# A two-layer mixer and expert trunk on one core: elementwise work goes from POOL to VectorE and ScalarE, the second layer's router sums move among the first layer's experts, and the first gather is split between the first expert products

## The chip, the cores and the metric

The kernel runs on one core of one Trainium2 chip. The core's engines work in parallel and each takes its own instructions in order: TensorE (PE; its weight loads are listed apart as PEld), VectorE (DVE), ScalarE (ACT), GpSimd (POOL) and SyncE (SP), which here issues the large transfers to 16 DMA engines. An instruction waits on semaphores for what it needs, and everything queued behind it on its engine waits too. The metric is device time in microseconds (us), the median of three runs: 862.81 us (861.21 to 863.67). A difference of 0.3% is about what a measurement of this kernel can tell.

## What is computed

Two layers over 256 tokens of 1024 channels, all in float32. A layer projects its input, runs four token mixers, gates and merges them, normalises, and then sends each token to two of 32 experts. Cut to what matters here:

```python
for l in range(DEPTH):                                   # 2 layers
    z = h @ w_in[l]                                      # 1024 -> 2560 + 4 * 1024 gate logits
    branches = (short_conv(sc_b, sc_c, sc_x, ...),       # gated convolution
                rg_lru(lru_x, ...),                      # recurrence over the tokens
                spatial_gating(sg_u, sg_v, ...),         # standardised in groups of 64, then a causal product
                retention(r_q, r_k, r_v, r_g, ...))      # rotated q and k, standardised output, silu gate
    merged = sum(sigmoid(gate_logits[b]) * (branches[b] @ branch_proj[l, b]) for b in range(4))
    mix = merged @ w_out[l]
    h = layer_norm(ALPHA * h + mix, ln_mix_g[l], ln_mix_b[l])
    ffn = hier_moe(h, ...)    # router: group by softmax, top 2 of its 8 experts; expert: silu(h wg) * (h wu) wd
    h = layer_norm(ALPHA * h + ffn, ln_ffn_g[l], ln_ffn_b[l])
```

## The kernel before

Weights come in chunks of 1 MB, 34 for a layer's mixers and 96 for its experts (8 groups of 4 experts, 12 chunks each: 8 for gate and up, 4 for down). A ring of 22 slots of 1 MB holds the chunks in flight and a few larger buffers. `Ring.pump` issues the next load from SyncE whenever a slot has been given back; the loads go out in the fixed order of the list, with a few others hung before certain chunks (`before`): the mixers' parameters `par` and the router's `rp` come before chunk 4 of layer 2.

**Mixers.** The products must be exact to float32, so each operand is split into a high half (ScalarE's cast, L256) and the rest (VectorE's subtraction, L257), and three products take the place of one (L328 to L330). A quarter of a chunk, 128x512, is a *piece*. A layer's mixers have 136, numbered from 0: ten chunks of input projections (q, k, lx, v, g, sv, su, c, x, b), then gates, branch projections (`proj`) and output projections in turn. A piece is 12 products (6 in the output projections). Splits run four pieces ahead (LOOK): the split for piece u + 4 is issued after the products of piece u, into the slot of the low halves (`wlo`) that piece u has just left. So VectorE can't run further ahead than that.

The mixers themselves are generators: after each piece, `advance` takes every one of them a step further, to its next `yield`. What a generator issues in a step stands in the engines' queues right behind that piece. A `yield` more or less thus moves all of its later work by one piece of 12 products. `g_ret` (retention), `g_lru` (recurrence) and `g_sgu` (spatial gating) use `std64`, which standardises over groups of 64 columns; its inverse root is found by `rsqrt`, 12 small steps on POOL (L315 to L318) on eight columns. The larger elementwise operations that don't read PSUM stand on POOL: the rotation's sum (L573), the retention output's two products (L620, L621) ahead of its transposes (L628), the recurrence's (L663, L673), the spatial gating's subtraction (L537) and products (L697, L714) around its products `sv` (L705).

**Residual and router sums.** After the first gate `residual` scales h by ALPHA on POOL; in layer 2 it first loads the norm's gain and bias (`gb`), scales them, and multiplies and adds them to h: five operations of 1024 or 2048 columns on POOL. `g_router` then puts the norm's gain into the router's weights `wr` and sums them with TensorE (L286, L296).

**Norm and routing.** `norm_mix` adds the residual, transposes the sums, and finds the router's logits from the sums themselves; mean and deviation are put in afterwards (L835, L838). Both token halves' logits share one PSUM bank; VectorE copies one half (L824), ScalarE the other (L825). `route` picks groups and experts, and makes one-hot matrices.

**Experts.** For a group, `gather` makes the tokens' columns (`xg`, L1151) by products with the one-hot matrices, a half of the channels (4 blocks) a call and 2 blocks a step. The first group's gather stands ahead of the first expert product (L1052): three of its four steps, and the fourth behind the weight k = 3. Each `gu` product of a chunk gives its slot back to the ring.

## Time and profile before

| | |
|---|---|
| median of 3 runs | 862.81 us |
| span of the profiled execution, first to last instruction | 860.7 us |
| mean granted TensorE clock | 0.970 of full speed |
| busy: TensorE, its weight loads, VectorE, ScalarE, POOL | 92%, 70%, 45%, 37%, 14% |
| layer 1: mixers to about 225 us, experts to about 425 us | |
| layer 2: mixers to about 652 us, experts to about 850 us | |
| read from HBM | 278.85 MB, 325 GB/s over the span |

The profile is of one execution, whose own time besides the span isn't listed; the span is 2.1 us under the median. A busy share of 92% on TensorE doesn't say that TensorE is the bound throughout: records of waiting products overlap, and in the experts its weights arrive one at a time. A granted clock of 1.00 is 2.4 GHz, 0.50 is 1.2 GHz; values between are means over a window. A row's bracket says how long the engine sat idle ahead of it and what ended that.

### The profile page before, as it was taken

Reading aid. Unit: us, or ns where it says so; the run is one execution under the profiler, and the core shown is the slowest. Engines: PE = TensorE matmul, PEld = TensorE weight load, DVE = VectorE, ACT = ScalarE, POOL = GpSimd, SP = SyncE. Lnnn points to the kernel's source line nnn. Section 1 sums busy time; section 2 is a strip of 40 time slices with the busy share of each in tenths; the row PEclk is TensorE's granted clock in tenths of the full one; section 3 lists DMA queues with packets and bytes.
Section 4 is the critical chain, followed back from the end, with each engine's and each line's share of the span. In section 5 each row is a group of like instructions: output and inputs, shape, how many; then the busy total and the mean of one; then the engine's idle time right before and its main releaser. Section 6 shows DMA issues by size and latency. Waiting matters only on the chain.

```text
span 860.7 us, 15923 instructions
## 1 busy us (share of the span) xinstructions
PE 791.3 (92%) x6438; PEld 604.1 (70%) x6438; DVE 386.0 (45%) x732; ACT 317.3 (37%) x636; POOL 124.8 (14%) x153
## 2 busy tenths in 40 slices
PE   8999999999999999867889998999999999979794
PEld 7998999999656555422389988999995565544342
DVE  5778677466621111110386779665674211111004
ACT  6564444444523211110356633544444131112012
POOL 4526211011000000000131437110010000000001
PEclk9999999999999999988999999999999999997898
DMA  9986735557799999999997474555587999999994
GB/s 346 425 354 264 253 122 179 191 196 280 323 424 426 426 426 425 425 421 425 424 425 303 158 281 164 183 196 191 175 334 320 426 426 426 425 426 427 423 425 175
DMA packets 40823, 281.07 MB, mean 327 GB/s; under 512 B 4588, under 2 KB 4588, under 8 KB 7456
## 3 DMA queue, kind: packets, MB, share of 16 engines
q1 hardware_dynamic: 40320, 279.20, 80.9%
q8 instruction: 54, 0.88, 0.4%
q10 hardware_dynamic: 288, 0.52, 0.2%
q0 software_dynamic: 128, 0.19, 0.1%
q14 instruction: 33, 0.27, 0.1%
HBM read 278.85 MB, written 1.05 MB: 325 GB/s over the span
## 4 chain that ended last, share of the span: by engine, by line
PE 58%; DMA 27%; DVE 7%; ACT 2%; POOL 1%; issue 1%; SPq 0%; DVEq 0%; ACTq 0%; POOLq 0%
DMA w<-in_exps_dram 25%; PE z L328 9%; PE z L330 9%; PE z L329 9%; PE gu L1052 6%; PE xg L1151 3%; PE y L1102 3%; PE acc L1089 3%; DVE wlo L257 2%; PE pj L330 2%; PE pj L328 2%; PE pj L329 2%; PE acc L328 2%; PE acc L329 2%; PE acc L330 2%; DMA par<-in_par_dram 2%
## 5 line engine op out<-in xcount | busy, mean ns | idle before, releaser
L257 DVE TENSOR_TENSOR wlo<-w,whi 128x512 fp32r<-128x512 f32 x269 | 215.7, 825 | 115.7 <-ACT whi L256 71.6
L330 PE MATMUL z<-hThi,wlo 128*128 128x256 f32 x672 | 192.2, 286 | 3.2 <-DVE wlo L257 3.0
L328 PE MATMUL z<-hThi,whi 128*128 128x256 f32 x672 | 192.5, 286 | 0.4 <-ACT whi L256 0.4
L329 PE MATMUL z<-hTlo,whi 128*128 128x256 f32 x672 | 191.3, 285 | 0.0
L256 ACT CAST whi<-w 128x512 fp32r<-128x512 f32 x272 | 151.4, 618 | 13.4 <-PE z L329 6.7
L1052 PE MATMUL gu<-w,xg 128*32 128x512 f32 x1024 | 128.0, 635 | 22.2 <-PEq L1175 13.0
L330 PEld LDWEIGHTS z<-hThi,wlo 128*128 128x128 f32 x672 | 130.1, 194 | 4.9 <-DVE wlo L257 4.9
L328 PEld LDWEIGHTS z<-hThi,whi 128*128 128x128 f32 x672 | 130.3, 194 | 1.2 <-ACT whi L256 0.7
L329 PEld LDWEIGHTS z<-hTlo,whi 128*128 128x128 f32 x672 | 130.2, 194 | 0.2
L1052 PEld LDWEIGHTS gu<-w,xg 128*32 128x32 f32 x1024 | 30.4, 114 | 98.2 <-issue 65.3
L1157 ACT ACTIVATE xg<-xg,cst 128x128 f32<-128x128 f32 x64 | 25.8, 454 | 167.2 <-PE xg L1151 163.9
L1159 DVE TENSOR_SCALAR xg<-xg,cst 128x128 f32<-128x128 f32 x64 | 23.3, 405 | 129.7 <-PE xg L1151 129.7
L1102 PE MATMUL y<-w,hidT 128*32 128x256 f32 x1024 | 65.4, 383 | 12.8 <-ACT hidT L1082 10.8
L1151 PEld LDWEIGHTS xg<-oh,h 128*128 128x128 f32 x512 | 59.6, 191 | 24.4 <-issue 22.7
L1089 PE MATMUL acc<-y,ct 128*128 128x256 f32 x256 | 68.1, 398 | 1.0 <-ACT y L1106 1.0
L1151 PE MATMUL xg<-oh,h 128*128 128x128 f32 x512 | 65.4, 281 | 0.0
L1089 PEld LDWEIGHTS acc<-y,ct 128*128 128x128 f32 x256 | 44.7, 189 | 25.0 <-issue 11.9
L1102 PEld LDWEIGHTS y<-w,hidT 128*32 128x32 f32 x1024 | 28.9, 109 | 41.1 <-ACT hidT L1082 14.6
L488 POOL TENSOR_TENSOR late<-late 128x512 f32<-128x512 f32 x16 | 25.9, 1616 | 203.9 <-DVE late L483 184.7
L1128 DVE TENSOR_TENSOR ow<-oh,wt 128x256 f32<-128x256 f32 x16 | 6.8, 424 | 106.9 <-PE y L1102 78.8
L1106 ACT COPY y<-y 128x256 f32<-128x256 f32 x64 | 23.8, 373 | 78.6 <-PE y L1102 78.6
L401 ACT ACTIVATE late<-z 128x512 f32<-128x512 f32 x32 | 19.1, 597 | 90.6 <-PE z L330 90.6
(257 smaller groups left out, 1044.4 us busy)
## 6 DMA issues: line engine op xcount, KB each, us to landing
w<-in_exps_dram SPq DMA_DIRECT2D x190, 1024.0 KB, 19.5
w<-in_mixw_dram SPq DMA_DIRECT2D x66, 1024.0 KB, 8.0
w<-in_mixw_dram SPq DMA_DIRECT2D x8, 256.0 KB, 6.2
par<-in_par_dram SPq DMA_DIRECT2D x2, 1024.0 KB, 15.9
w<-in_exps_dram SPq DMA_DIRECT2D x4, 512.0 KB, 17.7
xT<-in_xT_dram SPq DMA_DIRECT2D x4, 256.0 KB, 5.4
h<-in_xtok_dram SPq DMA_DIRECT2D x1, 1024.0 KB, 18.2
gb<-in_fgb_dram SPq DMA_DIRECT2D x1, 1024.0 KB, 5.8
```

The costliest lines, as they stand in the source:

```text
L256: self.nc.scalar.copy(hi, src)
L257: (eng or self.nc.vector).tensor_sub(lo, src, hi.bitcast(F32))
L328: nc.tensor.matmul(out, ah, bh, start=first and i == 0, stop=False, skip_group_check=True)
L329: nc.tensor.matmul(out, ah, bl, start=False, stop=False, skip_group_check=True)
L330: nc.tensor.matmul(out, al, bh, start=False, stop=stop_last and i == n - 1, skip_group_check=True)
L488: nc.gpsimd.tensor_add(a, a, pr)
L1052: nc.tensor.matmul(bank[32 * c:32 * c + 32], xg[g][k // 4][:, k % 4, 32 * c:32 * c + 32], w[:, c], start=k == 0, stop=k == 7, skip_group_c ...
L1089: nc.tensor.matmul(self.W[t][half][:, c0:c0 + 256], ct[:, t * P:t * P + P], y, start=g == 0 and c0 == 0, stop=g == 7, skip_group_check=True)
L1102: nc.tensor.matmul(bank[32 * c:32 * c + 32], hidT[:, f * P + 32 * c:f * P + 32 * c + 32], w[:, f, c], start=f == 0, stop=f == 1, skip_grou ...
L1106: nc.scalar.copy(ys[q], bank)
L1151: nc.tensor.matmul(bank[:, i * P:i * P + P], self.h[:, t, k * P:k * P + P], oh[:, t].rearrange("p e s -> p (e s)"), start=t == 0, stop=t == 1)
L1157: nc.scalar.activation(x[:, 2 * j + i], bank[:, i * P:i * P + P], AF.Identity, bias=b, scale=g)
```

## The change

- *POOL's large operations in the mixers* go to VectorE: L537, L573, L620 and L621 (in the other order), L663, L673, L697, L714. With them some `yield`s go: the retention transposes stand two pieces earlier, and so do the `sv` products.
- *The residual* becomes a generator, `g_residual`. Layer 1: four scalings of 512 columns on ScalarE, one a piece. Layer 2: the load at the same place, 14 pieces later four scalings of `gb` on ScalarE, then eight operations of 512 columns on VectorE, one every two pieces; the slot of `gb` is given back at its end.
- *Layer 2's router sums* run after group 6 of layer 1's experts, in PSUM banks of another kind. Their parameters `rp` are loaded ahead of chunk 56 of layer 1's experts, no more among layer 2's mixer chunks.
- *Routing*: the two halves' logits get a bank each, ScalarE copies both; mean and deviation are put together (`lm`) ahead of the logits, one step instead of two behind them; the value `nm` is made on POOL.
- *First gather*: two steps ahead of the first expert product, one each behind the weights k = 0 and k = 1.

The change also drops comments. The core of it:

```diff
+            before[(l - 1) * NCH + NMIX + 56] = [(self.router_params, l)]
...
                         if (j, bp) == (0, 0):
-                            self.residual(l)
-                            self.gens.append(self.g_router(l))
-                        if (j, bp) == (4, 0) and l:
-                            ring.give()
+                            self.mgens.append(self.g_residual(l))
+                            if l == 0:
+                                self.gens.append(self.g_router(l))
...
-        (nc.gpsimd if d is src else nc.vector).tensor_tensor(v3(d), v3(src), s[:, :, None].to_broadcast([P, 8, 64]),
-                                                             op=OP.subtract)
-        yield
-        if d is src:
-            yield
+        nc.vector.tensor_tensor(v3(d), v3(src), s[:, :, None].to_broadcast([P, 8, 64]), op=OP.subtract)
+        yield
...
-            nc.gpsimd.tensor_add(A, A, B)
+            nc.vector.tensor_add(A, A, B)
...
-        yield
-        nc.gpsimd.tensor_tensor(v3(d), v3(d), rs[:, :, None].to_broadcast([P, 8, 64]), op=OP.mult)
-        nc.gpsimd.tensor_mul(d, d, sl)
-        for _ in range(4):
+        nc.vector.tensor_mul(d, d, sl)
+        yield
+        nc.vector.tensor_tensor(v3(d), v3(d), rs[:, :, None].to_broadcast([P, 8, 64]), op=OP.mult)
+        for _ in range(2):
             yield
...
-        nc.gpsimd.tensor_mul(i, i, xc)
+        nc.vector.tensor_mul(i, i, xc)
...
-        nc.gpsimd.tensor_mul(r, r, i)
-        yield
+        nc.vector.tensor_mul(r, r, i)
...
-        nc.gpsimd.tensor_tensor(v3(vg), v3(vg), rs[:, :, None].to_broadcast([P, 8, 64]), op=OP.mult)
-        for _ in range(3):
+        nc.vector.tensor_tensor(v3(vg), v3(vg), rs[:, :, None].to_broadcast([P, 8, 64]), op=OP.mult)
+        for _ in range(2):
             yield
...
-        nc.gpsimd.tensor_mul(o, o, ug)
-        yield
+        nc.vector.tensor_mul(o, o, ug)
...
-        rb = self.bank("B", "rt")
+        rbt = [self.bank("W", "rt")[:, :P] for _ in range(2)]
...
-        self.stats_end(0)
+        self.recip(0)
         self.stats_var(1)
-        self.stats_end(1)
-        lt = self.tt("lt", [P, T])
-        nc.vector.tensor_copy(lt[:, :P], rb[:, :P])
-        nc.scalar.copy(lt[:, P:], rb[:, P:256])
+        lt = [self.tt("lt", [P, P]) for _ in range(2)]
+        for t in range(2):
+            nc.scalar.copy(lt[t], rbt[t])
...
         for t in range(2):
-            nc.vector.scalar_tensor_tensor(lm[:, t], self.rbs[:, 0], self.mv[:, t, 0:1], raw[:, t],
+            nc.vector.tensor_scalar(lm[:, t], self.rbs[:, 0], self.mv[:, t, 0:1], None, op0=OP.mult)
+        self.recip(1)
+        for t in range(2):
+            nc.vector.scalar_tensor_tensor(lm[:, t], lm[:, t], self.rs[:, t:t + 1], self.rbs[:, 1],
                                            op0=OP.mult, op1=OP.add)
-        for t in range(2):
-            nc.vector.scalar_tensor_tensor(lg[:, t], lm[:, t], self.rs[:, t:t + 1], self.rbs[:, 1],
+            nc.gpsimd.tensor_scalar(self.nm[:, t:t + 1], self.mv[:, t, 0:1], -1.0, None, op0=OP.mult)
+            nc.gpsimd.tensor_mul(self.nm[:, t:t + 1], self.nm[:, t:t + 1], self.rs[:, t:t + 1])
+        for t in range(2):
+            nc.vector.scalar_tensor_tensor(lg[:, t], raw[:, t], self.rs[:, t:t + 1], lm[:, t],
                                            op0=OP.mult, op1=OP.add)
...
+    def g_residual(self, l):
...
         if l == 0:
-            nc.gpsimd.tensor_scalar(self.h, self.h, ALPHA, None, op0=OP.mult)
+            for i in range(4):
+                yield
+                nc.scalar.mul(rows[:, 512 * i:512 * i + 512], rows[:, 512 * i:512 * i + 512], ALPHA)
             return
...
-        nc.gpsimd.tensor_scalar(gb, gb, ALPHA, None, op0=OP.mult)
-        for t in range(2):
-            nc.gpsimd.tensor_mul(self.h[:, t], self.h[:, t], gb[:, :1024])
-            nc.gpsimd.tensor_add(self.h[:, t], self.h[:, t], gb[:, 1024:])
+        for _ in range(14):
+            yield
+        for i in range(4):
+            nc.scalar.mul(gb[:, 512 * i:512 * i + 512], gb[:, 512 * i:512 * i + 512], ALPHA)
+            yield
+        for i in range(4):
+            c = slice(512 * (i % 2), 512 * (i % 2) + 512)
+            x = rows[:, 512 * i:512 * i + 512]
+            nc.vector.tensor_mul(x, x, gb[:, c])
+            yield
+            yield
+            nc.vector.tensor_add(x, x, gb[:, 1024 + c.start:1024 + c.stop])
+            yield
+            yield
+        self.ring.give()
...
-        next(first[1])
...
-                if (g, k) == (0, 3):
+                if g == 0 and k < 2:
                     next(first[1], None)
...
+            if g == 6 and l + 1 < L:
+                for _ in self.g_router(l + 1, "B"):
+                    pass
```

Where the changed file's line numbers differ, its rows below carry its own. VectorE in layer 1's mixers, from the variance of the spatial gating (`sbs`) to the transposed retention rows: before, five splits in a row and then the short convolution.

```order
L545 TENSOR_REDUCE sbs<-sgu 128x8
L546 TENSOR_SCALAR sbs<-sbs 128x8
L311 TENSOR_SCALAR ris<-sbs 128x8
L312 TENSOR_SCALAR rys<-ris 128x8
L257 TENSOR_TENSOR wlo<-w,whi 128x512 x5
L727 TENSOR_TENSOR sc<-z,sc 128x512
```

In the changed kernel, the same place on VectorE:

```order
L546 TENSOR_REDUCE sbs<-sgu 128x8
L547 TENSOR_SCALAR sbs<-sbs 128x8
L316 TENSOR_SCALAR ris<-sbs 128x8
L317 TENSOR_SCALAR rys<-ris 128x8
L258 TENSOR_TENSOR wlo<-w,whi 128x512 x2
L620 TENSOR_TENSOR ret_238<-ret_238 128x512
L258 TENSOR_TENSOR wlo<-w,whi 128x512
L622 TENSOR_TENSOR ret_238<-ret_238,ryr 128x512
L258 TENSOR_TENSOR wlo<-w,whi 128x512 x2
L697 TENSOR_TENSOR sgu<-sgu,rys 128x512
```

Three products that POOL had stand between the splits now; two of them read POOL's inverse roots (ryr, rys). The same engine a little earlier, from the retention's standardisation (`sar`) on; before:

```order
L537 TENSOR_TENSOR ret_238<-ro,sar 128x512
L672 SCALAR_TENSOR_TENSOR lru<-lru 128x512
L257 TENSOR_TENSOR wlo<-w,whi 128x512 x2
L545 TENSOR_REDUCE sbr<-ret_238 128x8
L546 TENSOR_SCALAR sbr<-sbr 128x8
```

In the changed kernel:

```order
L541 TENSOR_TENSOR ret_238<-ro,sar 128x512
L673 SCALAR_TENSOR_TENSOR lru<-lru 128x512
L674 TENSOR_TENSOR lru<-lru 128x512
L258 TENSOR_TENSOR wlo<-w,whi 128x512
L677 SCALAR_TENSOR_TENSOR lru<-lru 128x256 x2
L258 TENSOR_TENSOR wlo<-w,whi 128x512
L546 TENSOR_REDUCE sbr<-ret_238 128x8
```

The recurrence's product (L674) and its scans (L677) have moved ahead of the variance `sbr`. TensorE at the start of layer 1's experts, gather (`xg`) and the first products (`gu`); before:

```order
L1151 MATMUL xg<-oh,h 128x128 x12
L1052 MATMUL gu<-w,xg 32x512 x16
L1151 MATMUL xg<-oh,h 128x128 x4
L1052 MATMUL gu<-w,xg 32x512 x8
L1151 MATMUL xg<-oh,h 128x128 x8
```

In the changed kernel:

```order
L1173 MATMUL xg<-oh,h 128x128 x8
L1071 MATMUL gu<-w,xg 32x512 x4
L1173 MATMUL xg<-oh,h 128x128 x4
L1071 MATMUL gu<-w,xg 32x512 x4
L1173 MATMUL xg<-oh,h 128x128 x4
L1071 MATMUL gu<-w,xg 32x512 x16
```

The first expert product stands behind 8 gather products instead of 12 (each is two records in the trace, 16 instead of 24).

## Rows read from the trace of the kernel before

**Rows 1.** The page, part 2: GB/s in 40 equal slices of the span.

```profile
GB/s 346 425 354 264 253 122 179 191 196 280 323 424 426 426 426 425 425 421 425 424 425 303 158 281 164 183 196 191 175 334 320 426 426 426 425 426 427 423 425 175
```

**Rows 2.** The chain of waits, 330 to 440 us: start, us, what.

```profile
336.28 19.53 DMA w<-in_exps_dram
...
439.19 0.12 PE z L328
```

**Rows 3.** Windows of 1 us: PE, PEld, DVE, ACT, POOL busy, clock, DMA share, GB/s.

```profile
234.00:235.00 1.00, 1.00 (x14) 0.27 (x10) 0.09 (x1) 0.97 (x3) 0.00 (x0) 1.00 0.00 0
235.00:236.00 1.00, 1.00 (x16) 0.38 (x12) 0.00 (x0) 1.00 (x1) 0.00 (x0) 1.00 0.83 123
```

**Rows 4.** Timeline of TensorE and SyncE, start of layer 1's experts: start, us, what.

```profile
230.40 2.92 PE L1151 MATMUL xg<-oh,h 128*128 128x128 f32 x24
233.25 3.21 PE L1052 MATMUL gu<-w,xg 128*32 128x512 f32 x28
...
234.38 5.84 SPq L116 DMA_DIRECT2D w<-in_exps_dram  x6
```

**Rows 5.** Timeline of TensorE's weight loads in the mixers.

```profile
64.17 0.19 PEld L330 LDWEIGHTS z<-hThi,wlo 128*128 128x128 f32 x1 [0.44 <-DVE wlo L257]
...
73.78 0.42 PEld L628 LDWEIGHTS rtp<-cst,ret 128*128 128x128 f32 x4 [2.31 <-POOL ret L621]
...
89.15 0.19 PEld L330 LDWEIGHTS z<-hThi,wlo 128*128 128x128 f32 x1 [0.65 <-DVE wlo L257]
...
529.48 0.19 PEld L330 LDWEIGHTS z<-hThi,wlo 128*128 128x128 f32 x1 [1.30 <-DVE wlo L257]
```

**Rows 6.** Windows of 2 and of 10 us in the mixers, columns as above.

```profile
76.00:78.00 2.00, 2.00 (x11) 2.00 (x11) 1.34 (x2) 0.00 (x0) 1.23 (x2) 0.50 0.00 0
...
150.00:160.00 10.00, 10.00 (x85) 10.00 (x85) 4.14 (x7) 3.97 (x9) 0.00 (x0) 1.00 0.61 210
...
520.00:530.00 10.00, 8.77 (x71) 8.37 (x70) 9.88 (x7) 4.48 (x9) 9.76 (x5) 1.00 0.34 120
```

**Rows 7.** Timeline of VectorE, then POOL, in layer 1's mixers.

```profile
56.44 2.47 DVE L257 TENSOR_TENSOR wlo<-w,whi 128x512 fp32r<-128x512 f32 x2
...
63.42 2.14 DVE L257 TENSOR_TENSOR wlo<-w,whi 128x512 fp32r<-128x512 f32 x2
66.22 0.69 DVE L257 TENSOR_TENSOR wlo<-w,whi 128x512 fp32r<-128x512 f32 x1 [0.66 <-ACT whi L256]
...
68.05 3.10 DVE L257 TENSOR_TENSOR wlo<-w,whi 128x512 fp32r<-128x512 f32 x5
...
60.21 0.51 POOL L315 TENSOR_TENSOR rzr<-ryr 128x8 f32<-128x8 f32 x1 [1.84 <-DVE ryr L312]
60.79 0.50 POOL L316 TENSOR_TENSOR rzr<-rzr,sbr 128x8 f32<-128x8 f32 x1
...
75.41 0.20 POOL L316 TENSOR_TENSOR rzs<-rzs,sbs 128x8 f32<-128x8 f32 x1
...
84.54 5.75 POOL L922 TENSOR_SCALAR h<-h 128x2048 f32<-128x2048 f32 x1
```

**Rows 8.** The chain of waits in layer 2's mixers: the router sums.

```profile
511.40 1.02 PE rb L286 x16
516.92 0.56 PE rb L296 x4
```

**Rows 9.** A weight load in group 7; then the DMA issues, KB and us to landing.

```profile
397.75 0.16 PEld L1052 LDWEIGHTS gu<-w,xg 128*32 128x32 f32 x8 [1.70 <-DMA w<-in_exps_dram]
...
rp<-in_rp_dram SPq DMA_DIRECT2D x1, 384.5 KB, 15.7
```

**Rows 10.** Timeline of ScalarE and VectorE at layer 1's routing.

```profile
225.55 0.27 ACT L825 COPY lt<-rt 128x128 f32<-128x128 f32 x1 [0.68 <-DVE lt L824]
...
226.32 0.42 DVE L835 SCALAR_TENSOR_TENSOR lm<-rbs,mv,lg 128x40 f32<-128x40 f32 x2 [0.86 <-PE lg L828]
...
227.00 0.28 DVE L940 MAX8 top<-lg 128x8 f32<-128x8 f32 x2
```

More of the change, by code (lines that the diff above doesn't have):

```diff
@@ L257, in hilo, with router_params @@
         (eng or self.nc.vector).tensor_sub(lo, src, hi.bitcast(F32))
+    def router_params(self, l):
+        rp = self.lp.tile([P, 769], F32, name="rp")
+        self.nc.sync.dma_start(rp, self.a["rp"][l])
+        self.bsb = rp[:, :256].rearrange("p (c t) -> p c t", c=2)
+        self.wr = rp[:, 256:768].rearrange("p (k e) -> p k e", k=8)
+        self.rb = rp[:, 768:]
     def params(self, l):
-        nc, a, lp = self.nc, self.a, self.lp
+        nc, a = self.nc, self.a
         par = self.ring.take("par")
@@ L268, in params @@
         nc.sync.dma_start(par, a["par"][l])
-        rp = lp.tile([P, 769], F32, name="rp")
-        nc.sync.dma_start(rp, a["rp"][l])
-        self.bsb = rp[:, :256].rearrange("p (c t) -> p c t", c=2)
-        self.wr = rp[:, 256:768].rearrange("p (k e) -> p k e", k=8)
-        self.rb = rp[:, 768:]
+        if l == 0:
+            self.router_params(l)
     def done_with_params(self):
@@ L278, in done_with_params, with g_router @@
             self.ring.give()
-    def g_router(self, l):
+    def g_router(self, l, tag="W"):
         nc = self.nc
         gb = self.col(l, "mg", 0, 16).rearrange("p (i k) -> p i k", i=2)
-        bank = self.bank("W", "rb")
+        bank = self.bank(tag, "rb")
         for k in range(8):
@@ L293, in g_router @@
         yield
-        bank = self.bank("W", "rb")
+        bank = self.bank(tag, "rb")
         for i in range(2):
@@ L403, in mixer @@
                         if (j, bp) == (0, 0):
-                            self.residual(l)
-                            self.gens.append(self.g_router(l))
-                        if (j, bp) == (4, 0) and l:
-                            ring.give()
+                            self.mgens.append(self.g_residual(l))
+                            if l == 0:
+                                self.gens.append(self.g_router(l))
                         if (j, bp) == (7, 1):
@@ L764, in stats_var, with recip @@
         nc.scalar.activation(self.sd[:, t:t + 1], self.mv[:, t, 1:2], AF.Sqrt, bias=self.eps)
+    def recip(self, t):
+        self.nc.vector.reciprocal(self.rs[:, t:t + 1], self.sd[:, t:t + 1])
     def stats_end(self, t):
         nc = self.nc
-        nc.vector.reciprocal(self.rs[:, t:t + 1], self.sd[:, t:t + 1])
+        self.recip(t)
         nc.vector.scalar_tensor_tensor(self.nm[:, t:t + 1], self.mv[:, t, 0:1], -1.0, self.rs[:, t:t + 1],
@@ L797, in logits @@
                 o = i % 2 * 64
-                nc.tensor.matmul(rb[o:o + 64, t * P:t * P + P], self.wr[:, 4 * q + i], xT[t, q][:, i],
-                                 start=t + q == 0 and i < 2, stop=q == 1 and i > 1, skip_group_check=True)
+                nc.tensor.matmul(rbt[t][o:o + 64, :], self.wr[:, 4 * q + i], xT[t, q][:, i],
+                                 start=q == 0 and i < 2, stop=q == 1 and i > 1, skip_group_check=True)
         for t in range(2):
@@ L819, in norm_mix @@
         self.stats_add(1, 1, part(1, 1))
-        self.stats_end(0)
+        self.recip(0)
         self.stats_var(1)
-        self.stats_end(1)
-        lt = self.tt("lt", [P, T])
-        nc.vector.tensor_copy(lt[:, :P], rb[:, :P])
-        nc.scalar.copy(lt[:, P:], rb[:, P:256])
+        lt = [self.tt("lt", [P, P]) for _ in range(2)]
+        for t in range(2):
+            nc.scalar.copy(lt[t], rbt[t])
         raw = self.bank("W", "lg")[:, :80].rearrange("p (t e) -> p t e", t=2)
         for t in range(2):
-            nc.tensor.matmul(raw[:, t], lt[:, t * P:t * P + P], self.cst[:, C_SEL:C_SEL + 40], start=True, stop=True)
+            nc.tensor.matmul(raw[:, t], lt[t], self.cst[:, C_SEL:C_SEL + 40], start=True, stop=True)
         yield
@@ L915, in norm_ffn @@
             self.do_split(u)
-    def residual(self, l):
+    def g_residual(self, l):
         nc = self.nc
         self.needs[self.layer] -= 1
+        rows = self.h.rearrange("p t c -> p (t c)")
         if l == 0:
-            nc.gpsimd.tensor_scalar(self.h, self.h, ALPHA, None, op0=OP.mult)
+            for i in range(4):
+                yield
+                nc.scalar.mul(rows[:, 512 * i:512 * i + 512], rows[:, 512 * i:512 * i + 512], ALPHA)
             return
```

## The prediction

> **What bounds the kernel now.** I read the slices first, and in them the transfer rate [rows 1]: two flat stretches at 421 to 427 GB/s, slices 12 to 21 and 31 to 39, and between them 120 to 335 GB/s. So the core is bound in turn by two things. The chain of waits agrees: from 336.28 us it is one transfer of expert weights after another, 19.53 us each from issue to landing with eight in flight, while in the mixers it is one TensorE product after another, 0.12 us apart [rows 2]. A piece of weights (a quarter of a 1 MB chunk, 12 products) is therefore 12 x 0.12 = 1.44 us of TensorE.
>
> How the two join is in the 1 us windows at the start of layer 1's experts [rows 3]: at 234 us nothing moves, at 235 us the stream is back, and from there it stays full until the layer's weights are in. The ring of 22 slots is full when the mixers end. SyncE's next load is issued at 234.38 us, after the first expert product has given a slot back [rows 4]. So the end of a layer is this restart plus a fixed number of chunks. **Any time by which the first expert product comes earlier, in either layer, comes off the total one for one; anything that TensorE gains later in the experts is lost, and a byte added to the stream costs its transfer.**
>
> Then I looked for what TensorE loses ahead of the restart. The waits of its weight loads [rows 5] show: 0.44 us for a low half (wlo) of a piece; 2.31 us at the transposes of L628, for POOL's product L621; 0.65 us for another wlo behind POOL's 5.75 us residual [rows 7]. Layer 2 repeats the first two (0.36 and 2.30), and instead of 0.65 it has 0.34, 1.30 and 1.31 us, of which 1.30 is shown. After the 2.31 us of idleness the granted clock is 0.50 at 76 to 78 us, that is 1.2 GHz, and 0.72 and 0.93 in the two-microsecond windows before and behind it (only the middle one is shown); after the gaps of 0.34 and 1.30 us that lie between 526 and 530 us it stays at 1.00 [rows 6].
>
> **The change part by part.** *Mixers, pieces 28 to 39.* Before, one such stretch loses 0.44 + 2.31, some 0.25 at another wlo, and to the clock 2 x 0.28 + 2 x 0.50 + 2 x 0.07 = 1.7: 4.7 us. What is left of it? VectorE takes a split in 0.61 us (five of them in 3.10) [rows 7], and the operations taken from POOL have the same shape, 128x512, so 0.61 each. Ahead of piece 32's split VectorE gains L674 and L541, 1.22 us, and loses the stretching of a split beside POOL (two splits in 2.47 instead of 1.29: 1.2) [rows 7]. So wlo of piece 32 stays late by about 0.5. Next, split 35, which starts at 68.05, comes some 0.8 earlier: VectorE gains 0.85 (two splits in 2.14) and 0.66 (idle at 66.22, since ScalarE's square waited for POOL) [rows 7], and loses 0.1 to the step before and one cast, 0.6, that now stands behind that square. From 67.25 on, split 35, L620, split 36 and L622 end at 67.25 + 3 x 0.61 + 0.68 = 69.8 us. But the transposes now stand behind piece 34, not 36, and TensorE is there two pieces ahead of 73.78 - 2.31 = 71.47, at about 68.5: a wait of 1.3, bounds 0.5 to 2.0. On the pieces between I take 0.1. At the sv products, two pieces later, L697 should be done. Left: 0.5 + 0.1 + 1.3 = 2.0 (1.1 to 3.0), without a slow clock since no wait is over 1.3. Gain 4.7 - 2.0 = 2.7 a layer, **5.4**.
>
> *Residual.* In layer 1 it becomes four ScalarE scalings, one a piece; 0.65 goes. In layer 2 four scalings on ScalarE and eight operations on VectorE, one every two pieces: 0.61 + 0.61 / 2 = 0.9 of the 1.44 us of a piece. VectorE is 4.14 us of 10 busy in such a stretch [rows 6], so this is covered, and 0.34 + 1.30 + 1.31 = 2.95 goes. If the cover were gone it would cost 8 x 0.61 = 4.9. **3.6** together. The gb load keeps its place on SyncE's queue.
>
> *Other moves.* Rotations and the recurrence's products stand between 21 and 50 us, where the weight loads show no wait for VectorE that counts; cover is VectorE's idleness there, the price without it 0.61 each.
>
> *Router sums of layer 2.* TensorE loses 1.02 + 0.56 us [rows 8] from the mixers: **1.6**. Among the experts they stand ahead of group 7, whose second weight waits 1.70 us for its transfer anyway [rows 9]; the next waits are as long, so the 1.6 us, and a small VectorE step that the second half waits for, are hidden there. The parameters rp that they need now sit in the stream of expert weights, 384.5 KB [rows 9]: 0.394 MB / 426 GB/s = 0.92 us, **-0.9**. Before, they came behind the expert weights and cost nothing.
>
> *Routing.* ScalarE's copy of the second half of the logits stood 0.68 us idle for VectorE's copy L824 of the first [rows 10]. With both on ScalarE the first copy (0.27) goes into this gap: 0.68 - 0.27 = 0.41 earlier. Of the four small steps between L835 at 226.32 and L940 at 227.00 two are made ahead: 0.34. POOL's four small steps for nm feed only ScalarE's rows, which are ready some 1.2 us before the gather. 0.75 a layer, **1.5** (0 to 2).
>
> *First gather.* 24 rows of products in 2.92 us ahead of the first expert product [rows 4]; now 16: 8 x 0.122 = 0.97 a layer, **1.9**. The second slot then comes 1.9 us behind the first, and a chunk takes 1.048 MB / 426 GB/s = 2.46, so the stream isn't broken. Bounds 0 and 1.9.
>
> The sum: 5.4 + 3.6 + 1.6 - 0.9 + 1.5 + 1.9 = 13.1 us. The profiled execution's span is 860.7; with the 2.1 us by which the median is longer: 860.7 - 13.1 + 2.1 = **849.7 us**.
>
> **A rule against it.** One of POOL's 24 small steps for the two inverse roots (eight columns) takes 0.51 us and is 0.58 behind the one before while VectorE is at work, and 0.20 when VectorE waits [rows 7]. The Trainium skill (SBUF — State Buffer, Who interferes with whom) says that a VectorE operation with both inputs in SBUF and a GpSimd operation that reads SBUF exclude each other for a whole instruction. So the moved products hold up the very chain for which they wait. The trace agrees in direction (0.51 against 0.20). By the rule a step waits up to one VectorE operation, some 0.8 us in all, an estimate; by it the second chain would end so late that rival 2 is the forecast.
>
> **The rivals.** *1, nothing is left of the stalls.* VectorE keeps up through pieces 28 to 39: 2 x 2.0 more, 845.7 us. For it: the queue is stretched only beside POOL. Against: it adds as much ahead of piece 32 as it loses.
>
> *2, VectorE waits for POOL's roots.* The products L622 and L697 wait in VectorE's queue for the two chains, and the splits of the next pieces stand behind them. Two chains are 24 x 0.58 = 13.9 us from about 60.9 (60.21 and one more operation ahead), so 74.8, past the 73.8 of now. TensorE would wait as long as before and its clock fall again: the 5.4 is lost, 855.1 us. For it: the rows under load. Against: VectorE, when it waits, lets POOL go at 0.20.
>
> *3, the restart isn't moved by the first product,* because the slot that SyncE waits for is another: 849.7 + 1.9 = 851.6 us. Against: 234.38 lies right behind that product.
>
> *4, slower: VectorE becomes the bound of the mixers.* It takes on 18 operations in the two layers and 8 for the residual, 26 x 0.61 = 15.9 us. If wlo had no lead anywhere, all of it would be TensorE's; the residual's gain of 3.6 would go too, and 1.6 - 0.9 + 1.5 + 1.9 = 4.1 and the 2 x (2.3 + 1.7) at L628 would stay: 862.8 - 12.1 + 15.9 = 866.6 us. It decides from the point at which VectorE's work passes 1.44 us a piece; at 0.4 to 0.5 busy in the gates it doesn't.
>
> **How the numbers follow.** The forecast has 0.62, with 847 to 852 of its own; rival 1 0.13, rival 2 0.17, rival 3 0.05, rival 4 0.03. The range of 845.5 to 856 takes in all but rival 4 and the far ends. 0.3% is 2.6 us, about what a measurement of this kernel tells from no change: below 860.2 is faster. The cases up to 855.1 hold 0.97; with a wider error in rival 2, 0.94 faster, 0.03 the same, 0.03 slower.
>
> **What would show it.** In the changed profile: the wait at the transposes under 1.5 us and the clock at 1.00 through the mixers; no split on VectorE over 1.8 us in layer 2's first gates; the first expert product 16 rows of gather after the routing; the windows without transfer at the start of the experts some 1.7 us shorter; the full stretch in layer 1 longer by 0.9. It is wrong if the wait at L628 has only moved to a VectorE product, if the clock drops at another place, or if TensorE waits for wlo in the gates with VectorE over 0.9 busy.

## The result, and the profile after

| | kernel before | changed kernel |
|---|---|---|
| median | 862.83 us | 852.82 us |
| profiled execution, span | 860.7 us | 851.5 us |
| ratio to before, 95% interval | | 0.9885 (0.9871 to 0.9899) |

It is faster, by 10.0 us in the median; 13.1 had been forecast (849.7). The time lies in the range, and 0.8 us outside the forecast's own 847 to 852. The two profiled executions differ by 9.2 us, and this is where. The starts are those of the same TensorE instruction in both traces (a piece is 12 products):

| up to | before, us | after, us | ahead | this stretch | forecast |
|---|---|---|---|---|---|
| piece 31, layer 1 | 62.09 | 61.88 | 0.21 | +0.21 | 0 |
| piece 40 | 81.33 | 78.55 | 2.78 | +2.57 | 2.7 |
| end of the mixers | 221.72 | 218.21 | 3.51 | +0.73 | 0.65 |
| last sum of the experts | 425.20 | 421.42 | 3.78 | **+0.27** | 0.75 + 0.97 - 0.9 = 0.8 |
| piece 16, layer 2 | 458.24 | 456.48 | 1.76 | **-2.02** | 0 |
| piece 31 | 486.30 | 484.53 | 1.77 | 0.0 | 0 |
| piece 40 | 505.48 | 501.21 | 4.27 | +2.50 | 2.7 |
| piece 52 (router sums gone) | 524.72 | 519.02 | 5.70 | +1.43 | 1.6 |
| end of the mixers | 648.23 | 639.43 | 8.80 | +3.10 | 2.95 |
| last sum of the experts | 850.47 | 841.14 | 9.33 | **+0.53** | 0.75 + 0.97 = 1.7 |

So the mixers did what was worked out for them, within 0.2 us a line. Three lines did not, in bold. The weight loads that answer to [rows 5], with the wait in brackets at the end:

```profile
64.02 0.19 PEld L335 LDWEIGHTS z<-hThi,wlo 128*128 128x128 f32 x1 [0.51 <-DVE wlo L258]
67.19 0.19 PEld L335 LDWEIGHTS z<-hThi,wlo 128*128 128x128 f32 x1 [0.23 <-DVE wlo L258]
69.61 0.42 PEld L629 LDWEIGHTS rtp<-cst,ret 128*128 128x128 f32 x4 [1.17 <-DVE ret L622]
```

0.51 + 0.23 + 1.17 = 1.91 us is left of the stalls of pieces 28 to 39; the forecast had 0.5, 0.1 and 1.3, which add to 1.9 and stand there as 2.0. The windows that answer to [rows 6] (PE, PEld, DVE, ACT, POOL busy, clock, DMA share, GB/s) show no fall of the clock behind the transposes, and layer 2's first gates without a gap:

```profile
72.00:74.00 2.00, 2.00 (x26) 1.83 (x24) 1.73 (x4) 0.00 (x0) 0.20 (x1) 1.00 0.00 0
74.00:76.00 2.00, 2.00 (x19) 1.86 (x16) 2.00 (x4) 1.61 (x4) 0.00 (x0) 1.00 0.74 172
520.00:530.00 10.00, 10.00 (x86) 10.00 (x85) 6.47 (x11) 6.12 (x12) 1.26 (x1) 1.00 0.32 105
```

**The start of layer 2.** Here 2.0 us were lost for which no term stood. First the weight loads of after, then those of before, at piece 3 of layer 2, the first whose split VectorE makes (the three ahead of it are POOL's):

```profile
433.93 0.19 PEld L333 LDWEIGHTS z<-whi,hThi 128*128 128x128 f32 x1 [0.59 <-ACT whi L257]
435.41 0.19 PEld L334 LDWEIGHTS z<-wlo,hThi 128*128 128x128 f32 x1 [1.29 <-DVE wlo L258]
```

```profile
437.64 0.19 PEld L328 LDWEIGHTS z<-whi,hThi 128*128 128x128 f32 x1 [0.59 <-ACT whi L256]
438.69 0.19 PEld L329 LDWEIGHTS z<-wlo,hThi 128*128 128x128 f32 x1 [0.85 <-DVE wlo L257]
```

The wait for the first wlo has grown from 0.85 to 1.29 us. VectorE and POOL of after at that place, and below them the two in before:

```profile
434.24 2.93 DVE L258 TENSOR_TENSOR wlo<-w,whi 128x512 fp32r<-128x512 f32 x4
...
433.99 0.83 POOL L686 TENSOR_SCALAR_AFFINE_SELECT par<-par 128x512 f32<-128x512 f32 x1
```

```profile
437.95 3.08 DVE L257 TENSOR_TENSOR wlo<-w,whi 128x512 fp32r<-128x512 f32 x5
...
466.44 1.27 POOL L663 TENSOR_TENSOR lru<-lru 128x512 f32<-128x512 f32 x1 [15.60 <-ACT lru L661]
467.66 1.09 POOL L686 TENSOR_SCALAR_AFFINE_SELECT par<-par 128x512 f32<-128x512 f32 x1
```

POOL's mask of the gating weights (L686) used to stand in POOL's queue behind the rotations and the recurrence's product, and ran at 467 us, beside nothing that mattered. With those taken away it runs as soon as the queue is free, at 434 us, on top of VectorE's first splits: four of them take 2.93 us, where 4/5 of 3.08 is 2.46. Behind the longer wait the clock falls:

```profile
436.00:438.00 2.00, 2.00 (x13) 2.00 (x12) 1.82 (x4) 0.98 (x2) 0.00 (x0) 0.57 0.99 418
438.00:440.00 2.00, 2.00 (x12) 2.00 (x12) 0.73 (x3) 0.15 (x2) 0.00 (x0) 0.58 1.03 434
440.00:442.00 2.00, 2.00 (x19) 2.00 (x18) 1.92 (x5) 1.19 (x2) 0.00 (x0) 1.00 1.00 422
```

**The start of layer 1's experts,** which answers to [rows 3, 4]:

```profile
226.17 2.02 PE L1173 MATMUL xg<-oh,h 128*128 128x128 f32 x16
228.12 1.06 PE L1071 MATMUL gu<-w,xg 128*32 128x512 f32 x8
229.12 1.16 PE L1173 MATMUL xg<-oh,h 128*128 128x128 f32 x8
...
230.20 1.06 PE L1071 MATMUL gu<-w,xg 128*32 128x512 f32 x8
231.20 1.16 PE L1173 MATMUL xg<-oh,h 128*128 128x128 f32 x8
232.29 3.64 PE L1071 MATMUL gu<-w,xg 128*32 128x512 f32 x32
```

The gather starts 230.40 - 226.17 = 4.23 us earlier, 0.72 more than the mixers gave: that is the routing, forecast 0.75. The first expert product is 233.25 - 228.12 = 5.13 earlier, another 0.90: that is the split of the gather, forecast 0.97. But the next loads are issued at 229.25, 231.33 and 233.41 us, and the stream of weights stutters:

```profile
231.00:232.00 1.00, 1.00 (x11) 0.80 (x8) 0.04 (x1) 0.99 (x2) 0.00 (x0) 1.00 0.79 336
...
233.00:234.00 1.00, 1.00 (x12) 0.26 (x8) 0.00 (x0) 0.26 (x1) 0.00 (x0) 1.00 0.96 303
...
236.00:237.00 1.00, 1.00 (x10) 1.00 (x11) 0.00 (x0) 0.00 (x0) 0.00 (x0) 1.00 1.06 229
```

Before, from 237 us on, no window of this stretch is under 401 GB/s. What is left of the 5.13: the 56th expert load lands 321.53 - 317.96 = 3.57 us earlier, 0.06 ahead of the mixers' 3.51. The 57th, behind which rp now stands in the queue, lands 323.97 - 321.42 = 2.55 earlier, 1.02 less: that is rp, forecast 0.9. The 81st is 385.45 - 381.65 = 3.80 ahead; these 1.25 us came from a hitch in the profiled execution of before, and of the twelve runs below eleven gain 1.1 to 1.4 there, one 0.4, those that leave rp alone too.

### The profile page after: what moved, and what is told of

Its sections match the earlier page's. It is cut to its first block, busy times and chain, and to the rows that moved or that the text cites. A ratio compares the mean times of both kernels' runs of the same rounds, so it can differ in the third digit from the quotient of the medians.

```text
span 851.5 us, 15924 instructions
## 1 busy us (share of the span) xinstructions
PE 789.9 (93%) x6438; PEld 604.6 (71%) x6438; DVE 374.7 (44%) x756; ACT 322.0 (38%) x646; POOL 77.5 (9%) x137
## 3 DMA queue, kind: packets, MB, share of 16 engines
HBM read 278.85 MB, written 1.05 MB: 329 GB/s over the span
## 5 line engine op out<-in xcount | busy, mean ns | idle before, releaser
L258 DVE TENSOR_TENSOR wlo<-w,whi 128x512 fp32r<-128x512 f32 x269 | 191.5, 732 | 115.8 <-ACT whi L257 72.1
L1173 PE MATMUL xg<-oh,h 128*128 128x128 f32 x512 | 67.5, 286 | 0.0
L1108 PEld LDWEIGHTS acc<-y,ct 128*128 128x128 f32 x256 | 44.7, 189 | 25.0 <-issue 11.5
L333 PE MATMUL z<-whi,hThi 128*128 128x256 f32 x160 | 49.1, 307 | 2.3 <-ACT whi L257 2.3
```

What stands on the lines that cost most here:

```text
L258: (eng or self.nc.vector).tensor_sub(lo, src, hi.bitcast(F32))
L333: nc.tensor.matmul(out, ah, bh, start=first and i == 0, stop=False, skip_group_check=True)
L1108: nc.tensor.matmul(self.W[t][half][:, c0:c0 + 256], ct[:, t * P:t * P + P], y, start=g == 0 and c0 == 0, stop=g == 7, skip_group_check=True)
L1173: nc.tensor.matmul(bank[:, i * P:i * P + P], self.h[:, t, k * P:k * P + P], oh[:, t].rearrange("p e s -> p (e s)"), start=t == 0, stop=t == 1)
```

## The experiments

Executions of one kernel differ by microseconds, the changed one's from 851.86 to 853.42, those with the first gather whole from 850.04 to 854.26, and the traces differ by -1.3 to +1.3 us against before already at piece 16 of layer 1, where the edits do nothing yet. Steps of a microsecond are therefore read from starts in the traces, and the medians stand beside them.

### The first gather

Three runs: the changed kernel with the gather whole, the kernel before with the split alone, and the changed kernel with the split at another place.

```diff
+        next(first[1])
         weights = self.weights(l)
...
-                if g == 0 and k < 2:
+                if (g, k) == (0, 3):
```

> The changed kernel with one edit: the first gather as in the kernel before, three quarters ahead of the first expert product and the last quarter behind the fourth. Theory A (the split gives nothing that lasts: the first product is 0.97 us earlier, but the next two give their slots back 2.08 us apart instead of 0.86, the stream runs dry between them and starts its packets anew): no more than 0.7 us slower than the changed kernel, 852.3 to 853.5 us; the first issue of a load moves from 229.25 to about 230.2 us, the second to about 231.1, and from the ninth on the issues stand within 0.4 us of where they were. Rival (the split is worth the 1.9 us of the prediction and the shortfall lies elsewhere): 854.7 us.

Measured: 851.74 us, ratio 0.9881 (0.9863 to 0.9899). The time lies below both forecasts. Counted from the end of the mixers the first load goes out 0.89 us later than in the changed kernel, the second 0.33 us earlier, and nothing is lost by it: theory A.

```diff
-        next(first[1])
         weights = self.weights(l)
...
-                if (g, k) == (0, 3):
+                if g == 0 and k < 2:
```

> The kernel before with one edit: the first gather split as in the changed kernel (two quarters ahead of the first expert product, the others behind the first and the second). Theory A (the split gives nothing, or costs 0.2 us a layer in the stream): 862.8 to 863.5 us; the first expert product about 0.9 us earlier in each layer, the landings from the ninth restarted load on within 0.3 us of the kernel before. Rival (it is worth the 1.9 us of the prediction): 860.9 us.

Measured: 861.52 us, ratio 0.9994 (0.9985 to 1.0002). A gain of 1.9 us is outside this interval.

```diff
-                if g == 0 and k < 2:
+                if g == 0 and k in (1, 3):
```

> The changed kernel with one edit: the first gather's later quarters behind the second and the fourth expert product instead of the first and the second. Theory A (what the split earns is lost where single slots come back 2.08 us apart): the first product stays 1.62 us earlier than the end of the mixers gives, and now the stream keeps it: at equal bytes it stands 1.5 to 1.7 us ahead of the end of the mixers' gain in both layers (0.4 and 0.9 in the changed kernel, 0.75 and 0.9 with the whole gather), 1.6 us faster than the changed kernel in all, 851.2 us. Rival (the 1.6 us of the combined kernels came from the parameters' load or from the instruction fetches at the restart): 0.7 to 0.9 us in both layers, 852.5 us.

Measured: 849.53 us, ratio 0.9851 (0.9826 to 0.9877), lower still than expected. Its trace differs from the changed kernel's also by a fall of the clock that it doesn't have (1.5 us at the start of layer 2) and by 0.8 us ahead of piece 16 of layer 1, so the gather is read from the stream. The time from the end of the mixers until the trace's packets on the queue of weights reach 70 MB (layer 1) and 210 MB (layer 2) of the launch:

| kernel | quarters behind product | layer 1 | layer 2 |
|---|---|---|---|
| before | (three ahead) 4 | 32.91 us | 35.65 us |
| before, split alone | 1 and 2 | 33.15 | 35.88 |
| changed, gather whole | (three ahead) 4 | 32.14 | 34.79 |
| changed | 1 and 2 | 32.49 | 34.72 |
| changed, later quarters | 2 and 4 | 31.35 | 34.10 |

The split of the change is worth -0.35, +0.07, -0.24 and -0.23 us: nothing. The routing alone is worth 0.77 and 0.86. Behind the second and fourth product the split is worth 0.79 and 0.69, close to the 0.97 of the sum, and at equal bytes this run stands 1.56 and 1.55 us ahead of before, where theory A expected 1.5 to 1.7. Each figure is of one execution, and the runs further down tell how far such figures spread. Three more with the changed kernel's experts have 31.98 to 32.28 in layer 1 and 34.71 to 34.90 in layer 2, the gather whole has 35.84 in layer 2 of another kernel, and the experts of before have 34.14 in layer 1 of another. So in layer 2 the gain of the later quarters is clear (34.10 here, 33.97 and 34.04 in two kernels below, no other under 34.71); in layer 1 it is less so (with rp out of the stream too, 31.23 and 30.47 against 31.27 with the gather whole). In this run's timeline the first loads go out at 228.38 and 229.24 us, 0.86 apart:

```profile
227.25 1.92 PE L1071 MATMUL gu<-w,xg 128*32 128x512 f32 x16
228.38 7.07 SPq L116 DMA_DIRECT2D w<-in_exps_dram  x6
229.10 1.16 PE L1173 MATMUL xg<-oh,h 128*128 128x128 f32 x8
230.19 1.92 PE L1071 MATMUL gu<-w,xg 128*32 128x512 f32 x16
```

and the slices of 0.25 us of the ten microseconds from 230 us (changed) and from 229 us (later quarters) show the difference: after the first two microseconds the one has whole groups of slices under 300, the other single ones.

```profile
GB/s 131 360 0 0 0 492 426 426 295 393 426 459 426 361 197 229 360 426 426 426 393 426 426 426 295 197 229 197 131 393 492 426 459 328 328 426 492 361 361 459
```

```profile
GB/s 0 295 33 66 98 197 524 393 459 262 426 524 393 492 262 393 524 426 492 426 262 492 459 459 459 295 426 492 459 459 393 328 492 426 492 459 262 459 492 426
```

Over all kept traces, a microsecond under 300 GB/s that begins 15 to 21 us after the end of the mixers stands in all 12 layers of the kernels with the quarters behind 1 and 2, in one of 6 with 2 and 4, and in 2 of 10 with three quarters ahead. What makes the dip is not shown. The dip at 236.25 us in the changed kernel isn't a lack of loads, as theory A has it: the five issued from 229.25 to 235.13 us had none of them landed. Nor do these runs tell whether the spacing counts, or only that the second load goes out 11.89 us after the mixers instead of 13.12.

### The router's parameters

```diff
-            before[(l - 1) * NCH + NMIX + 56] = [(self.router_params, l)]
+            before[(l - 1) * NCH + NMIX + 22] = [(self.router_params, l)]
```

> The changed kernel with one edit: the load of the router's parameters for layer 2 (384.5 KB) stands ahead of the 23rd expert load of layer 1 instead of the 57th, so that it moves while the ring is full and the stream of weights stands still. Theory A (in the stream it costs its transfer): 0.9 us faster than the changed kernel, 851.9 us, and the landings of layer 1's expert weights no longer fall back by 1.0 us at the 57th. Rival (the stream is paced by its slowest queue and by the instruction fetches, and the 0.9 is lost in those steps): within 0.3 us, 852.8 us.

Measured: 851.85 us, ratio 0.9877 (0.986 to 0.9893). rp is issued at 221.83 us and has landed at 230.25, as the stream restarts. The 56th and the 57th expert load land 4.19 and 4.20 us ahead of before: the step of 1.02 is gone, and layer 1's experts, from the end of the mixers to the last sum, gain 2.20 us where the changed kernel gains 0.27. Theory A holds by the landings; the median can't tell, since the four kernels of one edit measured together lie between 851.74 and 852.13. Of the 1.9 us, 1.0 is rp; the rest lies in the restart, which differs from run to run.

### The mask on POOL

```diff
-        nc.gpsimd.affine_select(self.wsT, self.wsT, ...)      # first in g_sgu
...
         rs = yield from self.std64(bank, d, r1[1], "r")
+        nc.gpsimd.affine_select(self.wsT, self.wsT, ...)
```

> The changed kernel with one edit: POOL's mask of the gating weights (L686) is issued behind the first chain of roots, so that in layer 2 it no longer runs at 434 us beside VectorE's first splits. Theory A (with POOL's queue empty the mask moved up to there; it stretched four splits from 2.5 to 2.9 us, the wait for wlo grew from 0.86 to 1.29, and the clock fell to 0.50 behind it): the clock stays at 1.00 between 430 and 445 us, the first two pieces of layer 2 are 1.95 us shorter, 850.9 us. Rival (the clock falls there without the mask too, since TensorE stands idle for some 3 us between 428 and 436 in both kernels): the wait shrinks by 0.4, the clock falls all the same, 852.4 us.

Measured: 852.13 us, ratio 0.9878 (0.9861 to 0.9894). The wait at the first wlo is back, and so is the clock of 1.00:

```profile
434.87 0.19 PEld L334 LDWEIGHTS z<-wlo,hThi 128*128 128x128 f32 x1 [0.85 <-DVE wlo L258]
```

From piece 0 to 16 of layer 2 it is as fast as before (-0.02 us), where the changed kernel lost 1.96. But the mask now runs beside splits of pieces 31 to 35, and there 0.45 us a layer more is lost; so nothing is won in the time. Of the two parts of the 1.96, 0.44 is the mask: seven other runs with the mask up there lose 0.43 to 0.46 at this place. The other 1.5 is the clock, and it doesn't fall each time: it fell in the profiled execution of the changed kernel and in one of eight further ones with the mask there, and in none of the five without it. Two of nine against none of five doesn't tell whether the mask has a part in it.

### The waits at the transposes and the sv products

```diff
         nc.vector.tensor_tensor(v3(d), v3(d), rs[...], op=OP.mult)
-        for _ in range(2):
+        for _ in range(3):
             yield
```

> The changed kernel with one edit: the transposes of L629 stand one piece of weights (1.44 us) later. Theory A (the 1.17 us that TensorE waits there in each layer is only their place; VectorE is ahead again from the next piece on, wlo lies 2.3 us ahead): the wait goes without another in its place, 2 x 1.17 = 2.3 us, 850.5 us. Rival (VectorE is the bound of this stretch, so the wait moves to a wlo or to the sv products): within 0.5 us, 852.8 us.

Measured: 852.01 us, ratio 0.9877 (0.986 to 0.9893). The wait has moved, whole:

```profile
69.33 0.46 PEld L629 LDWEIGHTS rtp<-cst,ret 128*128 128x128 f32 x4
72.52 0.90 PEld L705 LDWEIGHTS sv<-par,sgu 128*64 128x64 f32 x16 [1.26 <-DVE sgu L697]
```

L697 waits in VectorE's queue for the second chain of roots:

```profile
71.77 0.69 DVE L697 TENSOR_TENSOR sgu<-sgu,rys 128x512 f32<-128x512 f32 x1 [1.50 <-POOL rys L323]
```

So my rival was right in the effect, and wrong in the engine: not VectorE's load, POOL's chain. The two waits have different causes. L622, for which the transposes wait, runs in a queue that has no idle time ahead of it (68.38 us here, the first chain done at 65.45); L697 waits for the second chain, in the changed kernel too, where TensorE came too late to notice. The next run moved both (the same edit at L697's loop as well).

> The changed kernel with two edits: the transposes of L629 and the products of L705 each one piece of weights (1.44 us) later. With the transposes alone moved, the wait of 1.17 us came back as 1.26 at L705, for L697, which waits for POOL's second chain of roots. Theory A (the chain of roots is the limit and ends at a fixed time, so both must stand behind it): no wait over 0.3 us at L629 and L705, 1.2 us gained in each layer, 2.4 us faster than the changed kernel, 850.4 us. Rival (the wait moves on, to the merging of the branches or a wlo in the first gates): within 0.5 us, 852.3 to 852.8 us.

Measured: 849.44 us, ratio 0.9856 (0.9841 to 0.987).

```profile
69.81 0.46 PEld L629 LDWEIGHTS rtp<-cst,ret 128*128 128x128 f32 x4
73.31 0.90 PEld L705 LDWEIGHTS sv<-par,sgu 128*64 128x64 f32 x16
```

No wait at either. Pieces 31 to 40 gain 3.74 and 3.70 us over before, where the changed kernel gains 2.57 and 2.50: 1.17 and 1.20 more, as expected. In layer 2 0.40 us of it is lost again at pieces 40 to 52, which gain 1.02 where the changed kernel's gain 1.42: one piece there waits 0.31 us for a cast and 0.51 for a split. So the rival is in it too.

### The parts alone

The kernel before, with only the mixers' operations on VectorE (std64, g_ret, g_lru and g_sgu of the change, the residual on POOL):

> The kernel before with one part of the change: the mixers' products, sums and differences of 128x512 go from POOL to VectorE, the residual stays on POOL. Theory A (this part is worth 2.57 and 2.52 us in pieces 31 to 40 of the two layers, and costs 0.44 at the start of layer 2, where the mask now finds POOL's queue empty): 862.8 - 5.1 + 0.4 = 858.1 us, the clock at 1.00 behind the transposes. Rival 1 (the mask came up for the sake of another part): 857.7 us, the mask of layer 2 where it was, at about 460 us. Rival 2 (VectorE's load makes the residual on POOL dearer, 5.75 us of it beside the splits): up to 2 us less gained, 860 us.

Measured: 860.4 us, ratio 0.9972 (0.9961 to 0.9983). Pieces 31 to 40 gain 2.56 and 2.51 us, the start of layer 2 loses 0.44, with the mask at 437.31 us: theory A in both. But rival 2 is in it too. POOL's residual starts now at 73.86 us, and lies beside the first gates' splits:

```profile
73.86 5.87 POOL L917 TENSOR_SCALAR h<-h 128x2048 f32<-128x2048 f32 x1
```

```profile
83.21 0.19 PEld L330 LDWEIGHTS z<-hThi,wlo 128*128 128x128 f32 x1 [1.14 <-DVE wlo L257]
85.39 0.19 PEld L330 LDWEIGHTS z<-hThi,wlo 128*128 128x128 f32 x1 [0.69 <-DVE wlo L257]
```

Pieces 40 to 46 lose 2.05 us against before. The residual alone (g_residual of the change, the mixers on POOL):

> The kernel before with one part of the change: the residual in pieces on ScalarE and VectorE, the mixers' products stay on POOL. Theory A (the terms of the two parts hang together: with the mixers' part alone the residual, still on POOL, cost TensorE 2.3 us at pieces 40 to 44 of layer 1 instead of 0.65, since VectorE's splits had lost their lead; alone the residual's part is worth what the trace of before shows, 0.65 + 2.95 = 3.6 us): 862.3 - 3.6 = 858.7 us. Rival (POOL's other work slows the new VectorE operations, or the mask or a product now runs beside them): 860 us or more.

Measured: 858.81 us, ratio 0.9952 (0.9936 to 0.9968). It gains 0.72 in layer 1 and 3.11 in layer 2 at the places of the sum, 3.83 for a forecast of 3.6. The parts are not additive: 2.05 of the residual's worth exists only once the mixers' operations have gone to VectorE.

This trace has something else to tell. In pieces 31 to 40 of layer 2, where it runs as before, it gains 1.06 us: TensorE waits 2.31 us at the transposes as before, but this time the clock stays at 1.00. Before, then this run:

```profile
498.00:500.00 2.00, 2.00 (x11) 2.00 (x12) 1.10 (x3) 0.00 (x0) 1.51 (x7) 0.53 0.75 299
```

```profile
498.32 0.42 PEld L626 LDWEIGHTS rtp<-cst,ret 128*128 128x128 f32 x4 [2.31 <-POOL ret L619]
502.22 0.90 PEld L703 LDWEIGHTS sv<-par,sgu 128*64 128x64 f32 x16 [0.58 <-POOL sgu L695]
499.00:501.00 2.00, 2.00 (x19) 2.00 (x19) 1.01 (x3) 0.00 (x0) 1.51 (x7) 1.00 0.45 188
```

With the split alone layer 2 shows the same: a wait of 2.31, no fall, 0.80 us of waiting at the sv products, a gain of 0.82. Of the six such stretches in the traces of before and of these two kernels the clock fell in four.

### Together

The gather whole, rp ahead of the 23rd load, transposes and sv one piece later:

> The changed kernel with four edits: the first gather whole, the router's parameters loaded ahead of layer 1's 23rd expert load, the transposes of L629 and the products of L705 one piece later. Theory A (the terms add: 2.4 for the waits, 0.95 for the parameters, 0.5 for the gather): 3.8 us faster than the changed kernel, 849.0 us; without a fall of the clock at the start of layer 2 some 1.5 us less still. Rival (the gains at the stream are lost in its steps again, and the waits move on): 852 us.

Measured: 848.54 us, ratio 0.9843 (0.9827 to 0.986). Layer 1's experts gain 2.0 us over the mixers' end, layer 2's lose 0.25: there the load behind the gap lands 0.53 us less ahead than the load before it, with a 16 KB instruction packet of 1.39 us among the restarting packets. That cause was not tried apart, and the stream dips once more there, as in layer 1 of the next kernel. The same with the later quarters behind the second and fourth product:

> The changed kernel with the transposes and the sv products one piece later, the router's parameters ahead of layer 1's 23rd expert load, and the first gather's two later quarters behind the second and the fourth expert product instead of the first and the second: the first two slots come back 0.86 us apart, and two loads are in flight at once. Theory A (the split gave nothing because single loads 2.08 us apart let the stream run dry): against the whole first gather the landings of layer 1 from the ninth restarted load on gain a further 0.6 to 0.9 us, 848.5 - 1.5 = 847 us. Rival (what TensorE does in all ahead of the sixth product sets the stream, whatever the order): the landings gain what they do with the whole gather, 0.7 to 0.9 us over the end of the mixers, 848.5 us.

Measured: 847.82 us, ratio 0.9823 (0.9805 to 0.9841), though its profiled execution lost 1.9 us at the start of layer 2. In layer 2 the experts gain 1.61 us, in layer 1 0.86, less than expected. And with the mask behind the second chain of roots:

> The kernel with the transposes and the sv products one piece later, the router's parameters in the gap and the gather's quarters behind the second and fourth product, and the mask of the gating weights issued behind POOL's second chain of roots. There POOL ends it at about 72.5 us, and the sv products come at 72.7. Theory A (the mask beside VectorE's first splits of layer 2 costs 0.44 us, and behind the roots nothing): 0.45 us less than without this edit, the first pieces of layer 2 without the 0.44. Rival (it runs beside L697 and stretches it, and the sv products wait 0.3 us in each layer): no gain.

Measured: **845.94 us**, ratio 0.9815 (0.9795 to 0.9834), the fastest here. The first pieces of layer 2 lose nothing, but each layer pays at the sv products what the rival said:

```profile
71.56 0.65 POOL L694 TENSOR_SCALAR_AFFINE_SELECT par<-par 128x512 f32<-128x512 f32 x1
```

```profile
72.86 0.90 PEld L705 LDWEIGHTS sv<-par,sgu 128*64 128x64 f32 x16 [0.29 <-issue]
```

0.16 us a layer in pieces 31 to 40, and 0.25 in pieces 40 to 44 of layer 2: by these rows the edit itself is worth nothing, but that the fall of the clock was not seen with it. The 1.9 us between the last two medians are not explained by it. The experts gain 2.81 and 1.58 us.

## Why the prediction was right, and where not

- **Bound, right.** What TensorE gained in the mixers came off the total nearly one for one: 3.51 and 8.80 us at the ends of the mixers, 3.78 and 9.33 at the ends of the layers. In the mixers or the residual alone, whose experts are those of before, the experts' own time differs from before by -1.2 to +0.7 us.
- **Stalls, right in the waits, lucky in the clock.** 1.91 us left a layer for 2.0 (its terms add to 1.9), gain 2.57 and 2.50 for 2.7, no slow clock behind them. The order of POOL's chain and the place of the transposes were read right; the wlo of piece 32 came 0.51 late for 0.5. But the 1.7 us a layer for the slow clock were read from one execution. Behind the same wait the clock stayed up in two of six stretches, which then took 18.36 and 18.13 us instead of before's 19.18; against those the change gains 1.5 to 1.7 us and not 2.5. And that no wait is over 1.3 us doesn't keep the clock up: at the start of layer 2 it fell behind one of 1.29.
- **Signs of being wrong, two of them seen.** The clock dropped at another place, the start of layer 2, and what is left at the transposes is a wait for a VectorE product, L622, though of 1.17 us and not 2.31.
- **Residual, right.** 0.73 and 3.10 for 0.65 and 2.95. That its price depends on the other part did not show in the sum, since both were made.
- **Router sums, nearly.** 1.43 for 1.6. The pieces behind them come earlier, and one now waits 0.48 us for a split (507.64 us) that the sums had covered.
- **rp, right.** 1.02 for 0.92, and avoidable: with it ahead of the 23rd load the step in the landings is gone.
- **Routing, right.** 0.72 a layer for 0.75, 0.77 and 0.86 in the stream.
- **First gather, wrong.** The step was "The second slot then comes 1.9 us behind the first, and a chunk takes 1.048 MB / 426 GB/s = 2.46, so the stream isn't broken". 2.46 us is a chunk's share of a full stream. The restarted one began with 15 packets of 1027 ns on average and then nothing new for three quarters of a microsecond, so that the first 1.05 MB took 3.5 us, and later it dipped to 303 and 229 GB/s in windows of 1 us. Of 1.9 us -0.28 arrived by bytes (-0.35 and +0.07, not clear of the spread), and in the landings of layer 1 no more. Why the later dips come is open. Rival 3 had the size of the loss, 851.6 us, by another mechanism: the restart was moved, and the gain lost behind it.
- **Start of layer 2, missing.** 1.96 us for which there was no term. I costed what the moved operations leave behind at their own places, and not what stood behind them in POOL's queue. 0.44 of it belongs to the change; the 1.5 of the clock was seen in two of nine executions with the mask there.
- **Rival 2, half right.** VectorE did stand for POOL's chain, 1.50 us at L697. TensorE did not, because in pieces 35 to 40 the splits lay 2.6 us and more ahead, and the transposes needed the first chain only. The rule weighed there, from the Trainium skill (SBUF — State Buffer, Who interferes with whom), agrees in direction again: of the second chain's steps the ones beside VectorE's work take 0.52 to 0.58 us, those while it waits 0.20. Both chains together took from 60.71 to 72.24 us, 11.5 us, where the slow rate gave 13.9.

Sum: 13.1 forecast; -2.2 first gather (1.9 + 0.28), -2.0 start of layer 2, -0.3 stalls, -0.1 rp, -0.2 router sums, +0.2 residual, +0.2 launch, +1.2 the hitch of before; 9.9 by these terms, and 9.2 in the spans. The 0.7 between lies in the landings of layer 1's experts and the end of layer 2; it is left open. The hitch and the fall of the clock belong to the two profiled executions and nearly cancel, which is luck.

## What to carry to other kernels

Here an earlier first load was kept, in layer 2 clearly, when the second slot came back 0.86 us behind the first, and lost when it came 2.08 us behind: in such a restart, release two slots close together, then do the other work. Whoever takes an operation out of an in-order queue must look at what stood behind it, since that moves up, and may land beside the critical engine. A wait that is taken away brings its engine earlier to the next operand, which may be late for another cause: here both the transposes and the sv products had to move. And what a slow clock costs in one execution may be absent in the next, and may hide another wait.

## What the hardware showed

A load that found the DMA idle began slowly: 8 KB packets took 309 ns in the full stream, and in the half microsecond from 651.0 us, the first behind layer 2's gap, four of them took 1195 ns on average; in the dip, from 657 us, again 687 ns. Instruction packets of 16 KB move at the same time: mostly 0.88 to 0.97 us each, in the hitch of before 1.58 and 2.01, and the landings of the loads there stood up to 4.04 us apart, where 2.44 is the median. That the packets cause this isn't shown. And the clock: behind the same wait of 2.30 to 2.31 us it fell to 0.50 in four of six stretches and stayed at 1.00 in two.
